# Gate matrix, top-k selection and sort of a PEER layer in 16-bit one-hot rows, and first gathers issued at seven places

## The chip, the cores and the metric

The kernel runs on one core of one Trainium2 chip. The metric is the device time of one execution in microseconds (us). A core has TensorE (PE, with its weight loads listed apart as PEld), VectorE (DVE), ScalarE (ACT), GpSimd (POOL) and SyncE (SP), which run their own instruction lists in order and wait for each other through semaphores, and 16 DMA engines that move data between HBM and the on-chip memory.

## The reference

One layer of a streaming encoder, over 256 positions of width 2048, all in f32. Its first half (adaptive normalization, a short convolution, latent attention, an output projection) is not touched by the change. The second half is a product-key retrieval over 128 x 128 = 16384 experts of one neuron each:

```python
q = (h @ w_q).reshape(bsz, seq, PEER_HEADS, 2, PEER_QDIM // 2)        # 8 heads, 2 halves of 128
scores = jnp.einsum('bshpd,hpnd->bshpn', q, sub_keys)                 # 128 keys per half
top_v, top_i = lax.top_k(scores, 16)
cand = top_v[..., 0, :, None] + top_v[..., 1, None, :]                # 16 x 16 candidates
best_v, best_i = lax.top_k(cand.reshape(..., 256), 16)
i1 = take_along_axis(top_i[..., 0, :], best_i // 16); i2 = take_along_axis(top_i[..., 1, :], best_i % 16)
expert = i1 * 128 + i2
gate = softmax(best_v)
a = einsum('td,tnd->tn', hx, u_tab[expert])
out = einsum('tn,tnd->td', gelu(a) * gate, v_tab[expert])
```

So each token picks 8 x 16 = 128 experts (i1, i2) with a gate each. The layer ends in a residual sum and a normalization.

## The kernel before

The tables `peer_u` and `peer_v` are not gathered per token. The kernel multiplies all 16384 rows of `peer_u` with all 256 tokens, 128 rows ("a block", index i1) at a time, and multiplies the activations with a dense gate matrix G[i1, i2, token] that is zero except at the chosen experts. The second table is then read row by row in a sorted order, so that rows that few tokens use share a matmul.

**Order of the work.** The whole is one Python program whose instructions are put in order, engine by engine, by a planner that goes by priority and by its own estimate of times; an instruction that is not marked by `keep` may be moved ahead of others. After the first half (to about 580 us) the main loop (from line 1154) runs over the 128 blocks. A block loads 1 MB of `peer_u` (`ru`), splits it on ACT into a high part (`hu`, line 198) and on DVE into a low part (`lu`, line 199), both with a raised priority (line 192), and does 48 matmuls (`pu`, lines 213, 214, 217): 16 slices of the high part with both halves of h2, then 16 of the low part. The last 16 need `lu`. A GELU (line 1160) writes the block's activations to a tile of eight blocks (`A`).

**Side work.** Between blocks, `pay(x)` advances a generator whose steps yield what they cost; each block pays 3.3 (`SIDE`) for the first 48 blocks, then, from block 51 on, 2.4 (`SORT_SIDE`). What is left of a generator at block 48 is drained there.

- `side_steps`, blocks 0 to 48, for each half of the tokens (tt): the 256 candidates, their top 16 (`top16`), the lookup of i1 and i2 by a comparison with `iota` over 8 x 16 x 16 elements (`eq`, line 902), a multiplication (line 906) and a reduction (line 908), the softmax, and a transpose on PE into `i1T`, `i2T`, `gT` (lines 921 to 923), one column per token. Then the one-hot rows: `oh_make` compares `iota` with four tokens' indices at a time, [128 selections, 4 tokens, 128] in f32, for i2 (into `work`, three places in turn) and i1 (into a tile of tag `e2`, four buffers), and ACT multiplies the latter by the gate (line 847). `oh_use`, two steps later (`HOLD`), makes one 128x128x128 f32 matmul per token (line 857), and ACT moves four tokens to a `stage` (line 859), of 16 tokens each. A full stage is written to HBM (`gd`, line 862) and reduced to its maximum on DVE (lines 865, 868).
- `sort_steps`, from block 51: from the maxima it sorts the 128 x 128 rows by which groups of 32 tokens use them (`tri`, `rank`), and turns ranks into a permutation by one-hot rows again (lines 1060 to 1076, `invert`): 32 chunks, each of four 128x256 16-bit matmuls (line 1057). The result is `perm_idx`.
- `ask(k)` reads the gate matrix of eight blocks back (`gg`, line 1100), `weigh(k)` multiplies it onto the activations on DVE (line 1106) and writes them to HBM (`actd`, line 1111). The first `ask` is at block 48, the first `weigh` at block 51.

**After the loop.** GpSimd gathers rows of v (`rv`, line 1145, 1 MB each) and of the activations (`mc`, line 1152) by `perm_idx`, and PE multiplies them (`po`, lines 1203 and 1211). Seven of the gathers of v (`EARLY`) are issued in the loop, all at block 118 (`EARLY_AT`), where the sort's remaining steps are also drained; five use tiles of the tag `A` (seven buffers), two the place of `work`.

Of the kernel before, what the change touches and what calls it, by code (L numbers as in the profile page):

```python
# [31 lines left out]
E2BUFS = 4  # L32
HOLD = 2
WRAW = 4
# [19 lines left out]
AHEAD = 8  # L54
EARLY_AT = NBLK - 10
RAWS = 11
# [74 lines left out]
def hybrid_block_kernel(  # L131
# [34 lines left out]
    def ps_tile(name):  # L166
# [76 lines left out]
    with tc.tile_pool(name="pre", bufs=1) as pre:  # L243
# [3 lines left out]
        def t8(name, dt=F32, shape=(128, 8, 256)):  # L247
            return pre.tile(list(shape), dt, tag="t8", name=name, bufs=6)

        vec = pre.tile([128, NVEC], F32, name="vec")  # L250
        nc.sync.dma_start(vec, vecs)
# [529 lines left out]
    def g8(name, shape, dt=F32):  # L781
# [9 lines left out]
           for i in range(2)]  # L791
    sifs = [tks[:, 1024 + i * 256:1280 + i * 256].rearrange("p (h k) -> p h k", k=16) for i in range(2)]

    def m1(name, dt=F32):
        return sp.tile([128, 256], dt, tag="m1", name=name, bufs=5)

# [34 lines left out]

    i1T, i2T, gT = [m1(n) for n in ("i1T", "i2T", "gT")]
    work = cst.tile([128, 4096], F32, tag="T2", name="work")
# [3 lines left out]
    def oh_make(tt, q):  # L837
        t = tt * 128 + q * 4
        it = iota.unsqueeze(1).to_broadcast([128, 4, 128])
        ohs = []  # L840
        for i, src in enumerate((i2T, i1T)):
            oh = e2(f"oh{tt}_{q}") if i else work[:, 2048 + 512 * ((32 * tt + q) % 3):][:, :512]
            oh = oh.rearrange("p (t i) -> p t i", t=4)
            V.tensor_tensor(oh, it, src[:, t:t + 4].unsqueeze(2).to_broadcast([128, 4, 128]), ALU.is_equal)  # L844
            ohs.append(oh)
        for j in range(4):
            S.activation(ohs[1][:, j], ohs[1][:, j], AF.Copy, scale=gT[:, t + j:t + j + 1])  # L847
        return ohs

    def oh_use(tt, q, ohs):  # L850
        tb, qq = divmod(q, TB // 4)
        if qq == 0:
            stages[tt, tb] = g8(f"stage{tt}_{tb}", (128, 128, TB))
        stage = stages[tt, tb]
        p = ps_tile(f"gps{tt}_{q}")
        for j in range(4):
            keep(PE.matmul(p[:, j * 128:(j + 1) * 128], lhsT=ohs[0][:, j], rhs=ohs[1][:, j],  # L857
                          start=True, stop=True))
        S.activation(stage[:, :, qq * 4:(qq + 1) * 4].rearrange("p i t -> p t i"),
                     p.rearrange("p (t i) -> p t i", t=4), AF.Copy)  # L860
        if qq == TB // 4 - 1:
            S.dma_start(gd[tt * (128 // TB) + tb], stage)
            gm = picked[:, 4 * tt + tb * TB // 32]
            if tb * TB % 32 == 0:
                V.tensor_reduce(gm, stage, AX.X, ALU.max)
            else:
                mx = e2(f"mx{tt}_{tb}")[:, :128]
                V.tensor_reduce(mx, stage, AX.X, ALU.max)
                V.tensor_tensor(gm, gm, mx, ALU.max)

    def side_steps():
# [5 lines left out]
        for tt in range(2):  # L877
# [16 lines left out]
            for which in range(2):  # L894
                if which == 0:
                    V.tensor_single_scalar(bs, bi, 4, ALU.logical_shift_right)
                else:
                    V.tensor_single_scalar(bs, bi, 15, ALU.bitwise_and)
                bf = tk[:, 1536:1664].rearrange("p (h k) -> p h k", k=16)
                V.tensor_copy(bf, bs)  # L900
# [5 lines left out]
                V.tensor_tensor(eq, eq, sfv[:, :, which].unsqueeze(2).to_broadcast([128, 8, 16, 16]),  # L906
                                ALU.mult)
                V.tensor_reduce(sel[:, which], eq, AX.X, ALU.add)
                yield 4.4
# [10 lines left out]
            ts_ = slice(tt * 128, (tt + 1) * 128)  # L920
            V.tensor_copy(i1T[:, ts_], pt[:, 0:128])
# [35 lines left out]
    def sort_steps():  # L957
        nk = len(CLASSES) + 1
        cls = work[:, 2048:2048 + 64 * nk].bitcast(BF).rearrange("p (k i) -> p k i", k=nk)
        flat = sp.tile([128, 512], BF, tag="m1", name="tri", bufs=5)  # L960
        tri, ones_bf, tot = flat[:, 0:128], flat[:, 128:256], flat[:, 256:256 + nk]
# [84 lines left out]
        V.tensor_single_scalar(ri, ri, 127, ALU.bitwise_and)  # L1046
        plo = work[:, 1024:1280].rearrange("p (c i) -> p c i", c=2)
        V.tensor_copy(plo[:, 0], ri)
        V.tensor_copy(plo[:, 1], rj)
        yield 5.0  # L1050
        pi = ps_tile("inv")
        it = iota.unsqueeze(1).to_broadcast([128, 4, 128])
        late = None

        def invert(ch, oh, vals):
            for i in range(4):
                keep(PE.matmul(pi[:, :256], lhsT=oh[:, 0, i], rhs=vals[:, i].rearrange("p a b -> p (a b)"),
                              start=(ch == 0 and i == 0), stop=(ch == 31 and i == 3)))

        for ch in range(32):  # L1060
            isl = slice(ch * 4, (ch + 1) * 4)
            oh = sp.tile([128, 2, 4, 128], BF, tag="e2", name=f"sl{ch}", bufs=E2BUFS)
            vals = sp.tile([128, 4, 2, 128], BF, tag="e2", name=f"sv{ch}", bufs=E2BUFS)
            for i in range(2):
                V.tensor_tensor(oh[:, i], it, plo[:, i, isl].unsqueeze(2).to_broadcast([128, 4, 128]),
                                ALU.is_equal)
            V.tensor_scalar(vals[:, :, 0], oh[:, 1], pidx, None, ALU.mult)
            V.tensor_tensor(vals[:, :, 1], oh[:, 1], iota[:, isl].unsqueeze(2).to_broadcast([128, 4, 128]),
                            ALU.mult)
            if late is not None:  # L1070
                invert(*late)
            late = (ch, oh, vals)
            yield 2.4
        yield 2.4
# [79 lines left out]
    for i1 in range(NBLK):  # L1154
# [260 lines left out]
```

## Time and profile before

| | us |
|---|---|
| median of three runs | 1780.37 |
| lowest and highest of them | 1776.81, 1781.57 |
| the profiled execution | 1774.11 |
| its span, first to last instruction | 1771.5 |
| PE busy (share of the span) | 1679.7 (95%) |
| PEld, weight loads | 1461.9 (83%) |
| DVE | 1210.0 (68%) |
| ACT | 761.3 (43%) |
| POOL | 297.5 (17%) |

The profile is that of one execution. Busy time counts a matmul from its start to its modelled end; matmuls overlap, so a busy PE may still lose time between starts, and the distance of starts says what a matmul costs. In a row of a group stand line, engine, operation, output<-inputs, shape and count, then busy time in total and mean ns of one, then the idle time of the engine ahead of them and what ended it. A line of the timeline or of the chain of waits starts with the time from the span's start and the duration, both in us.

### The profile page before, as it was taken

What the parts mean: (1) busy time and instruction counts of PE and PEld (TensorE: products, weight loads), DVE (VectorE), ACT (ScalarE), POOL (GpSimd) and SP (SyncE); (2) the same over time, 40 slices, a digit from 0 to 9 for tenths busy, and PEclk for the clock granted to TensorE, in tenths of its full rate; (3) what the DMA queues carried; (4) which work ended last, traced back from release to release, by engine and by line L of the source; (5) the groups of instructions that cost most, each with busy time, mean ns of one, the idle gap of its engine ahead of it and who ended that gap; (6) DMA issues with size and microseconds to landing.
All of it is one profiled execution on the core that took longest, in us unless ns stands there. A gap on an engine that the chain in (4) does not pass through costs nothing.

```text
span 1771.5 us, 29562 instructions
## 1 busy us (share of the span) xinstructions
PE 1679.7 (95%) x12526; PEld 1461.9 (83%) x12526; DVE 1210.0 (68%) x1621; ACT 761.3 (43%) x1013; POOL 297.5 (17%) x257
## 2 busy tenths in 40 slices
PE   3777999999999999999999999999999999999996
PEld 2667999989999999899999999999999854444542
DVE  6667978979867898898876697898754232312424
ACT  3224356534544449856884433333333232312322
POOL 0000000000000000000001000000030377777771
PEclk8888999999999999999999999999999999999999
DMA  9986887869854555545659887878888699999895
GB/s 392 385 336 214 327 299 269 316 250 348 311 213 165 192 194 191 206 166 191 223 214 337 305 296 262 298 286 309 289 300 335 216 386 382 347 383 344 343 371 232
DMA packets 77928, 505.93 MB, mean 286 GB/s; under 512 B 9472, under 2 KB 10112, under 8 KB 22496
## 3 DMA queue, kind: packets, MB, share of 16 engines
q1 hardware_dynamic: 44784, 319.82, 48.4%
q0 software_dynamic: 29712, 162.94, 25.1%
q10 hardware_dynamic: 3296, 21.24, 3.0%
q8 instruction: 100, 1.64, 0.4%
q14 instruction: 36, 0.29, 0.0%
HBM read 466.21 MB, written 37.75 MB: 284 GB/s over the span
## 4 chain that ended last, share of the span: by engine, by line
PE 85%; DVE 7%; ACT 4%; DMA 2%; issue 1%; POOL 1%; POOLq 0%; SPq 0%; ACTq 0%; DVEq 0%
PE pu L213 13%; PE pu L214 13%; PE pu L217 13%; PE po L1203 11%; PE po L1211 6%; PE gps L857 2%; PE pwin L213 2%; PE pwin L214 2%; PE pq L213 2%; PE pq L217 2%; PE pq L214 2%; DVE lwin L199 2%; PE pwout L213 1%; PE pwin L217 1%; PE pwout L214 1%; PE pwout L217 1%
## 5 line engine op out<-in xcount | busy, mean ns | idle before, releaser
L213 PE MATMUL pu<-h2hi,hu 128*128 128x256 f32 x2048 | 497.8, 285 | 0.0
L198 ACT ACTIVATE hu<-ru 128x2048 fp32r<-128x2048 f32 x128 | 245.5, 1918 | 364.4 <-PE pu L214 310.4
L213 PEld LDWEIGHTS pu<-h2hi,hu 128*128 128x128 f32 x2048 | 385.9, 188 | 0.6 <-issue 0.2
L199 DVE TENSOR_TENSOR lu<-ru,hu 128x2048 fp32r<-128x2048 f32 x128 | 292.9, 2289 | 134.4 <-ACT hu L198 134.2
L217 PE MATMUL pu<-h2hi,lu 128*128 128x256 f32 x2048 | 263.0, 281 | 0.0
L217 PEld LDWEIGHTS pu<-h2hi,lu 128*128 128x128 f32 x2048 | 251.3, 189 | 0.0
L214 PE MATMUL pu<-h2loT3a,hu 128*128 128x256 f32 x1024 | 249.7, 282 | 0.0
L214 PE MATMUL pu<-h2loT3b,hu 128*128 128x256 f32 x1024 | 248.2, 281 | 0.0
L1203 PE MATMUL po<-rv,mc 128*64 128x512 f32 (+2 forms) x1064 | 219.9, 595 | 5.1 <-PEq L1285 2.6
L214 PEld LDWEIGHTS pu<-h2loT3a,hu 128*128 128x128 f32 x1024 | 193.8, 189 | 0.2 <-issue 0.2
L214 PEld LDWEIGHTS pu<-h2loT3b,hu 128*128 128x128 f32 x1024 | 193.6, 189 | 0.0
L1203 PEld LDWEIGHTS po<-rv,mc 128*64 128x64 f32 (+2 forms) x1064 | 69.3, 129 | 144.5 <-issue 136.3
L1100 POOL DMA_DIRECT2D gg<-gd x16 | 18.7, 1170 | 928.5 <-DMA gd<-stage 928.3
L1152 POOL DMA_INDIRECT mc<-actd,perm_idx x109 | 134.4, 1233 | 37.1 <-issue 30.8
L1145 POOL DMA_INDIRECT rv<-in_peer_v_dram,perm_idx x107 | 125.3, 1171 | 65.5 <-issue 25.3
L204 DVE TENSOR_TENSOR lv<-rv,hv 128x2048 fp32r<-128x2048 f32 x24 | 55.1, 2295 | 117.5 <-ACT hv L203 117.4
L241 DVE SCALAR_TENSOR_TENSOR acc<-ada,cact,acc 128x2048 f32<-128x2048 f32 x45 | 105.7, 2349 | 5.9 <-DMA ada<-in_w_ada_dram 5.9
L203 ACT ACTIVATE hv<-rv 128x2048 fp32r<-128x2048 f32 x24 | 45.9, 1913 | 125.6 <-DMA rv<-in_peer_v_dram,perm_idx 98.1
L198 ACT ACTIVATE hwin<-rwin 128x2048 fp32r<-128x2048 f32 x33 | 63.1, 1916 | 81.3 <-DMA rwin<-in_w_in_dram 46.1
L204 DVE TENSOR_TENSOR third<-rv,third 128x2048 fp32r<-128x2048 f32 x12 | 27.5, 2294 | 89.5 <-ACT third L203 89.5
L847 ACT ACTIVATE oh<-oh,gT 128x128 f32<-128x128 f32 x256 | 80.9, 392 | 14.8 <-DVE oh L844 14.1
L213 PE MATMUL pwin<-hhi,hwin 128*128 128x256 f32 x336 | 84.7, 293 | 0.0
(522 smaller groups left out, 3048.1 us busy)
## 6 DMA issues: line engine op xcount, KB each, us to landing
ru<-in_peer_u_dram SPq DMA_DIRECT2D x128, 1024.0 KB, 5.3
ada<-in_w_ada_dram SPq DMA_DIRECT2D x96, 1024.0 KB, 6.7
rwin<-in_w_in_dram SPq DMA_DIRECT2D x33, 1024.0 KB, 6.1
rwout<-in_w_out_dram SPq DMA_DIRECT2D x16, 1024.0 KB, 7.3
rwq<-in_w_q_dram SPq DMA_DIRECT2D x16, 1024.0 KB, 6.5
gd<-stage ACTq DMA_DIRECT2D x16, 1024.0 KB, 5.3
gg<-gd POOLq DMA_DIRECT2D x16, 1024.0 KB, 11.1
actd<-A POOLq DMA_DIRECT2D x15, 1024.0 KB, 6.3
```

Of the source, the lines that this page charges most:

```text
L198: S.activation(hi, raw, AF.Copy)
L199: V.tensor_tensor(lo, raw, hi.bitcast(F32), ALU.subtract)
L204: V.tensor_tensor(lo, src, hi.bitcast(F32), ALU.subtract)
L213: PE.matmul(dst, lhsT=whi[:, sl], rhs=rhi[:, c], start=(c == sets[0][0]), stop=False)
L214: PE.matmul(dst, lhsT=whi[:, sl], rhs=rlo[:, c], start=False, stop=False)
L217: PE.matmul(dst, lhsT=wlo[:, sl], rhs=rhi[:, c], start=False, stop=(c == sets[-1][-1]))
L241: V.scalar_tensor_tensor(acc, raw, cact[:, k:k + 1], acc, ALU.mult, ALU.add)
L847: S.activation(ohs[1][:, j], ohs[1][:, j], AF.Copy, scale=gT[:, t + j:t + j + 1])
L1145: keep(nc.gpsimd.indirect_dma_start(raw, None, v_rows, index(main[n])))
L1152: keep(nc.gpsimd.indirect_dma_start(ms[-1][:, n % 8], None, actd[:, :], index(main[n])))
L1203: keep(PE.matmul(po[tt * 4 + d4][row:row + size], lhsT=m[:, at * size:(at + 1) * size], rhs=raw[:, d4 * 512:(d4 + 1) * 512], start=start, ...
L1211: keep(PE.matmul(po[tt * 4 + d4], lhsT=m[:, mi, tt * 128:(tt + 1) * 128], rhs=r[:, d4 * 512:(d4 + 1) * 512], start=False, stop=False, skip ...
```

## The change

The one-hot rows become 16-bit (bfloat16, which holds the integers 0 to 127 exactly), eight tokens at a time. Indices are stored twice, side by side, so that the innermost dimension of each operand of a comparison is two adjacent 16-bit elements. The gate stays exact to f32 by being split into three 16-bit parts (`gT[..., 0..2]`): the one-hot row of i1 is multiplied by all three on DVE in one operation, and PE adds three 16-bit matmuls per token. The multiplication on ACT goes. `HOLD` is 1. The product `og` has two places in `work`, both one-hot rows are tiles of tag `e2`. The lookup in the top-k selection compares and multiplies in 16 bits too. In the sort, 16 chunks of eight replace 32 of four, with two matmuls of 128 columns where one had 256. `iota` is 16-bit and is made by a count and a cast. The seven first gathers of v are issued at blocks 114, 116, ... 126, one each, and the sort's rest is drained at 114. The yields change with the step sizes: 2.6 per eight tokens instead of 1.2 per four, 2.0 instead of 1.0 behind the transpose, 2.6 per chunk of eight in the sort instead of 2.4 per chunk of four.

```diff
-HOLD = 2
+HOLD = 1
+OHB = 8
...
-EARLY_AT = NBLK - 10
+EARLY_AT = (114, 116, 118, 120, 122, 124, 126)
...
-    iota = cst.tile([128, 128], F32, name="iota")
-    nc.gpsimd.iota(iota, pattern=[[1, 128]], base=0, channel_multiplier=0,
-                   allow_small_or_imprecise_dtypes=True)
+    iota = cst.tile([128, 128], BF, name="iota")
...
+        V.tensor_copy(iota, count[:, :128])
...
-    i1T, i2T, gT = [m1(n) for n in ("i1T", "i2T", "gT")]
+    i1T, i2T = [sp.tile([128, T, 2], BF, tag="m1", name=n, bufs=2) for n in ("i1T", "i2T")]
+    gT = sp.tile([128, T, 3, 2], BF, tag="gT", name="gT")
+
+    def pairs_of(x):
+        return x.rearrange("p (a b) -> p a b", b=2)
+
+    def hot(dst, idx):
+        n = idx.shape[1]
+        V.tensor_tensor(dst.rearrange("p n (a b) -> p n a b", b=2),
+                        pairs_of(iota).unsqueeze(1).to_broadcast([128, n, 64, 2]),
+                        idx.unsqueeze(2).to_broadcast([128, n, 64, 2]), ALU.is_equal)
+
+    def twice(x):
+        return x.unsqueeze(2).to_broadcast([128, x.shape[1], 2])
...
     def oh_make(tt, q):
-        t = tt * 128 + q * 4
-        it = iota.unsqueeze(1).to_broadcast([128, 4, 128])
-        ohs = []
-        for i, src in enumerate((i2T, i1T)):
-            oh = e2(f"oh{tt}_{q}") if i else work[:, 2048 + 512 * ((32 * tt + q) % 3):][:, :512]
-            oh = oh.rearrange("p (t i) -> p t i", t=4)
-            V.tensor_tensor(oh, it, src[:, t:t + 4].unsqueeze(2).to_broadcast([128, 4, 128]), ALU.is_equal)
-            ohs.append(oh)
-        for j in range(4):
-            S.activation(ohs[1][:, j], ohs[1][:, j], AF.Copy, scale=gT[:, t + j:t + j + 1])
-        return ohs
+        t = tt * 128 + q * OHB
+        oh2, oh1 = [e2(f"oh{i}_{tt}_{q}").bitcast(BF).rearrange("p (t i) -> p t i", t=OHB) for i in (2, 1)]
+        og = work[:, 1024 + 1536 * (q % 2):2560 + 1536 * (q % 2)].bitcast(BF).rearrange("p (t c i) -> p t c i", t=OHB, c=3)
+        hot(oh2, i2T[:, t:t + OHB])
+        hot(oh1, i1T[:, t:t + OHB])
+        V.tensor_tensor(og.rearrange("p t c (a b) -> p t c a b", b=2),
+                        oh1.rearrange("p t (a b) -> p t a b", b=2).unsqueeze(2).to_broadcast([128, OHB, 3, 64, 2]),
+                        gT[:, t:t + OHB].unsqueeze(3).to_broadcast([128, OHB, 3, 64, 2]), ALU.mult)
+        return oh2, og
...
         for j in range(4):
-            keep(PE.matmul(p[:, j * 128:(j + 1) * 128], lhsT=ohs[0][:, j], rhs=ohs[1][:, j],
-                          start=True, stop=True))
+            for c in range(3):
+                keep(PE.matmul(p[:, j * 128:(j + 1) * 128], lhsT=ohs[0][:, t0 + j], rhs=ohs[1][:, t0 + j, c],
+                              start=(c == 0), stop=(c == 2)))
...
-                eq = g8(f"eq{tt}_{which}", (128, 8, 16, 16))
-                V.tensor_tensor(eq, bf.unsqueeze(3).to_broadcast([128, 8, 16, 16]),
-                                iota[:, :16].unsqueeze(1).unsqueeze(1).to_broadcast([128, 8, 16, 16]),
-                                ALU.is_equal)
+                eq = g8(f"eq{tt}_{which}", (128, 8, 16, 16), BF)
+                V.tensor_tensor(eq.rearrange("p h k (a b) -> p (h k) a b", b=2),
+                                bf.unsqueeze(2).to_broadcast([128, 128, 8, 2]),
+                                pairs_of(iota[:, :16]).unsqueeze(1).to_broadcast([128, 128, 8, 2]), ALU.is_equal)
...
-            V.tensor_copy(i1T[:, ts_], pt[:, 0:128])
-            V.tensor_copy(i2T[:, ts_], pt[:, 128:256])
-            V.tensor_copy(gT[:, ts_], pt[:, 256:384])
-            yield 1.0
-            for q in range(32):
+            V.tensor_copy(i1T[:, ts_], twice(pt[:, 0:128]))
+            V.tensor_copy(i2T[:, ts_], twice(pt[:, 128:256]))
+            left = tk[:, 1792:1920]
+            V.tensor_copy(gT[:, ts_, 0], twice(pt[:, 256:384]))
+            V.tensor_tensor(left, pt[:, 256:384], gT[:, ts_, 0, 0], ALU.subtract)
+            V.tensor_copy(gT[:, ts_, 1], twice(left))
+            V.tensor_tensor(left, left, gT[:, ts_, 1, 0], ALU.subtract)
+            V.tensor_copy(gT[:, ts_, 2], twice(left))
+            yield 2.0
+            for q in range(128 // OHB):
...
-                yield 1.2
+                yield 2.6
...
         def invert(ch, oh, vals):
-            for i in range(4):
-                keep(PE.matmul(pi[:, :256], lhsT=oh[:, 0, i], rhs=vals[:, i].rearrange("p a b -> p (a b)"),
-                              start=(ch == 0 and i == 0), stop=(ch == 31 and i == 3)))
+            for i in range(8):
+                for a in range(2):
+                    keep(PE.matmul(pi[:, a * 128:(a + 1) * 128], lhsT=oh[:, i], rhs=vals[a][:, i],
+                                  start=(ch + i + a == 0), stop=(ch == 15 and i == 7), skip_group_check=True))
...
-        if i1 == EARLY_AT:
+        if i1 == EARLY_AT[0]:
             for _ in side:
                 pass
-            for n in range(EARLY):
-                fetch_raw(n)
+        if i1 in EARLY_AT:
+            fetch_raw(EARLY_AT.index(i1))
```

More of the change, by code (lines that the diff above doesn't have):

```diff
@@ L248, in t8 @@
             return pre.tile(list(shape), dt, tag="t8", name=name, bufs=6)
+        count = s2("count")
+        nc.gpsimd.iota(count[:, :128], pattern=[[1, 128]], base=0, channel_multiplier=0,
+                       allow_small_or_imprecise_dtypes=True)
+        V.tensor_copy(iota, count[:, :128])
         vec = pre.tile([128, NVEC], F32, name="vec")
@@ L791, in hybrid_block_kernel @@
            for i in range(2)]
-    sifs = [tks[:, 1024 + i * 256:1280 + i * 256].rearrange("p (h k) -> p h k", k=16) for i in range(2)]
-    def m1(name, dt=F32):
-        return sp.tile([128, 256], dt, tag="m1", name=name, bufs=5)
+    sifs = [tks[:, 1024 + i * 128:1152 + i * 128].bitcast(BF).rearrange("p (h k) -> p h k", k=16)
+            for i in range(2)]
     def e2(name):
@@ L837, in oh_make, with oh_use, oh_four @@
     def oh_make(tt, q):
-        t = tt * 128 + q * 4
-        it = iota.unsqueeze(1).to_broadcast([128, 4, 128])
-        ohs = []
-        for i, src in enumerate((i2T, i1T)):
-            oh = e2(f"oh{tt}_{q}") if i else work[:, 2048 + 512 * ((32 * tt + q) % 3):][:, :512]
-            oh = oh.rearrange("p (t i) -> p t i", t=4)
-            V.tensor_tensor(oh, it, src[:, t:t + 4].unsqueeze(2).to_broadcast([128, 4, 128]), ALU.is_equal)
-            ohs.append(oh)
-        for j in range(4):
-            S.activation(ohs[1][:, j], ohs[1][:, j], AF.Copy, scale=gT[:, t + j:t + j + 1])
-        return ohs
-    def oh_use(tt, q, ohs):
+        t = tt * 128 + q * OHB
[7 more added lines that the diff above has]
+        return oh2, og
+    def oh_use(tt, b, ohs):
+        for half in range(OHB // 4):
+            oh_four(tt, b * (OHB // 4) + half, ohs, 4 * half)
+    def oh_four(tt, q, ohs, t0):
         tb, qq = divmod(q, TB // 4)
@@ L959, in sort_steps @@
         cls = work[:, 2048:2048 + 64 * nk].bitcast(BF).rearrange("p (k i) -> p k i", k=nk)
-        flat = sp.tile([128, 512], BF, tag="m1", name="tri", bufs=5)
+        flat = sp.tile([128, 512], BF, tag="m1", name="tri", bufs=2)
         tri, ones_bf, tot = flat[:, 0:128], flat[:, 128:256], flat[:, 256:256 + nk]
@@ L1046, in sort_steps @@
         V.tensor_single_scalar(ri, ri, 127, ALU.bitwise_and)
-        plo = work[:, 1024:1280].rearrange("p (c i) -> p c i", c=2)
-        V.tensor_copy(plo[:, 0], ri)
-        V.tensor_copy(plo[:, 1], rj)
+        plo = work[:, 1024:1280].bitcast(BF).rearrange("p (c i b) -> p c i b", c=2, b=2)
+        V.tensor_copy(plo[:, 0], twice(ri))
+        V.tensor_copy(plo[:, 1], twice(rj))
         yield 5.0
         pi = ps_tile("inv")
-        it = iota.unsqueeze(1).to_broadcast([128, 4, 128])
+        iota2 = work[:, 1408:1536].bitcast(BF).rearrange("p (i b) -> p i b", b=2)
@@ L1053, in sort_steps @@
+        V.tensor_copy(iota2, twice(iota))
         late = None
         def invert(ch, oh, vals):
-            for i in range(4):
-                keep(PE.matmul(pi[:, :256], lhsT=oh[:, 0, i], rhs=vals[:, i].rearrange("p a b -> p (a b)"),
-                              start=(ch == 0 and i == 0), stop=(ch == 31 and i == 3)))
[L1060 to L1069, printed above, removed]
+            for i in range(8):
+                for a in range(2):
+                    keep(PE.matmul(pi[:, a * 128:(a + 1) * 128], lhsT=oh[:, i], rhs=vals[a][:, i],
+                                  start=(ch + i + a == 0), stop=(ch == 15 and i == 7), skip_group_check=True))
@@ new lines, in sort_steps @@
+        for ch in range(16):
+            isl = slice(ch * 8, (ch + 1) * 8)
+            flats = ([work[:, 2048 + 512 * n:2560 + 512 * n] for n in range(4)] if ch % 2 else
+                     [e2(f"s{n}{ch}") for n in range(4)])
+            oh, oj, *vals = [x.bitcast(BF).rearrange("p (i j) -> p i j", i=8) for x in flats]
+            hot(oh, plo[:, 0, isl])
+            hot(oj, plo[:, 1, isl])
+            V.tensor_scalar(vals[0], oj, pidx, None, ALU.mult)
+            V.tensor_tensor(vals[1].rearrange("p i (a b) -> p i a b", b=2),
+                            oj.rearrange("p i (a b) -> p i a b", b=2),
+                            iota2[:, isl].unsqueeze(2).to_broadcast([128, 8, 64, 2]), ALU.mult)
```

6 lines of the change are left out of this document (3 added, 3 removed).

## The prediction

> **What bounds the kernel now.** I read the list of costliest groups first, then busy time in windows, then the waits inside them, then the timeline, down to single bursts of matmuls.
>
> Two stretches build the gate matrix from one-hot rows, 657 to 759 us (first 128 tokens) and 810 to 926 us (second). The windows view of both:
>
> ```profile
> 657.00:759.00 102.00, 97.22 (x817) 96.05 (x815) 83.69 (x92) 88.21 (x179) 0.00 (x0) 1.00 0.57 205
> 810.00:926.00 116.00, 112.03 (x952) 111.27 (x952) 93.68 (x97) 98.75 (x192) 0.00 (x0) 1.00 0.60 212
> ```
>
> Columns: stretch, length, then busy time of PE, weight loads, DVE, ACT, POOL, then granted clock, DMA share, GB/s. The clock is full and DMA at 0.6, so neither limits. PE is busy 209.25 of 218 us and idle 8.75; DVE is busy 177.4 (81%), ACT 187.0 (86%). So TensorE sets the time here, and its idle time adds to it. What it waits for, and what DVE waits for, in the waits view from 657 to 926 us:
>
> ```profile
> PE gps L857 <- ACT oh L847: 8.7, 9, 1.8
> DVE lu L199 <- ACT hu L198: 17.5, 12, 3.4
> DVE work L844 <- PE gps L857: 14.4, 14, 3.2
> DVE mx L868 <- ACT stage L859: 4.9, 3, 2.6
> DVE work L865 <- ACT stage L859: 3.1, 5, 1.1
> ```
>
> (Columns: total in us, number of waits, longest.) All PE idle time there waits for one thing: the scaling of one-hot rows by the gate on ScalarE, line 847. Outside these stretches the `peer_u` blocks follow each other without gaps. The chain of waits has their last sixteen matmuls every 5.68 us:
>
> ```profile
> 592.27 1.89 PE pu L217 x16
> 597.95 1.89 PE pu L217 x16
> 669.89 2.68 PE gps L857 x24
> ```
>
> So each microsecond of matmul removed before 1402 us, where the last block ends, shortens the run. After it comes the expert product, fed by gathers of v; nothing of its matmuls changes.
>
> **The change part by part.**
>
> *One-hot matmuls.* Now, the groups:
>
> ```profile
> L857 PE MATMUL gps<-oh,work 128*128 128x128 f32 x512 | 67.4, 280 | 8.7 <-ACT oh L847 8.7
> L844 DVE TENSOR_TENSOR work<-iota,i2T 128x512 f32<-128x512 f32 x64 | 43.9, 688 | 14.4 <-PE gps L857 14.4
> L844 DVE TENSOR_TENSOR oh<-iota,i1T 128x512 f32<-128x512 f32 x64 | 43.2, 686 | 0.0
> L847 ACT ACTIVATE oh<-oh,gT 128x128 f32<-128x128 f32 x256 | 80.9, 392 | 14.8 <-DVE oh L844 14.1 <-ACT oh L847 0.7
> L906 DVE TENSOR_TENSOR eq<-eq,tks 128x2048 f32<-128x2048 f32 x4 | 9.2, 2288 | 0.0
> L1068 DVE TENSOR_TENSOR sv<-sl,iota 128x512 bf16<-128x512 bf16 x32 | 21.9, 685 | 0.0
> L1067 DVE TENSOR_SCALAR sv<-sl,pidx 128x512 bf16<-128x512 bf16 x32 | 11.3, 353 | 0.9
> L865 DVE TENSOR_REDUCE work<-stage 128x128 f32<-128x2048 f32 x8 | 18.3, 2284 | 3.1 <-ACT stage L859 3.1
> ```
>
> Each of 256 tokens is one f32 matmul, run as two instructions: 512. Mean durations overlap, so I take the distance of starts. In the chain 24 of them take 2.68 us: 0.1117 each, 57.2 us in all. After the change a token is three 16-bit matmuls of 128 columns: 768. The trace has this shape in the ranking of the sort, timeline from 1011.5 us:
>
> ```profile
> 1011.81 0.39 PE L1031 MATMUL rank<-work,tri 128*128 128x512 bf16 x1
> 1012.04 0.39 PE L1034 MATMUL rank<-tri 128*128 128x128 bf16 x4
> 1012.23 0.37 PE L213 MATMUL pu<-h2hi,hu 128*128 128x256 f32 x1
> 1012.44 0.28 PE L214 MATMUL pu<-h2loT3a,hu 128*128 128x256 f32 x1
> ```
>
> and the summary of that line (shortest, median, longest duration in ns):
>
> ```profile
> L1034 PEld LDWEIGHTS <-tri x24: 97/98/100, 1011.8 to 1048.8; 128*128 128x128 bf16 x24
> L1034 PE MATMUL rank<-tri x24: 219/220/220, 1012.0 to 1048.8; 128*128 128x128 bf16 x24
> ```
>
> Four take 0.39 us, the last alone 0.22, so starts are (0.39 - 0.22)/3 = 0.057 us apart, each with its own weight load. At that distance 768 take 43.8 us. It is a bound from below, since it is a run of only four, behind a long matmul that can hide a load. From above: a weight load lasts 98 ns, and if loads did not overlap 768 would take 75.3 us. I take 0.057, because the loads in that row do overlap.
>
> The Trainium skill speaks against it: "TensorE: Matmul & The Clock Gate", section Back-to-back issue gap, states about 81 ns per matmul for sustained pairs of load and matmul at 128 columns. By that figure the 768 would be an estimated 62 us, more than now. No row here shows a long run of this shape.
>
> The first f32 matmul behind 16-bit ones is late: from the last L1034 (1012.04 + 0.39 - 0.22 = 1012.21) to L214 at 1012.44 are 0.23 us, where 0.057 and one `peer_u` distance of 5.68/48 = 0.118 make 0.175. That is 0.055 per burst; at some 28 bursts, 1.5 us.
>
> *DVE in these stretches.* It loses 128 comparisons of 512 elements (43.9 + 43.2 = 87.1 us) and gains 64 comparisons of 1024 and 32 multiplications of 3072, all operands 16 bits. Between 512 elements (687 ns) and 2048 (2288 ns), a two-tensor operation costs 1.043 ns per further element. No row shows a two-tensor operation with only 16-bit operands. Upper bound, as f32: 1221 and 3357 ns. Lower: L1067, all 16 bits, takes 353 ns for 512 elements, half of 687; half the steps gives 687 and 1756 ns. I take the lower, as L1067 is the only row with 16 bits throughout. That makes 44.0 + 56.2 = 100.2 us, 13.1 more than now. The three copies behind the transpose become seven operations; a copy now is
>
> ```profile
> 658.95 0.28 DVE L921 COPY i1T<-selT 128x128 f32<-128x128 f32 x1
> ```
>
> and with doubled outputs some 0.4 each: about 2 us more per half, 4 in all. DVE then needs 177.4 + 13.1 + 4 = 194.5 us in stretches that PE would leave at 218 - 57.2 + 43.8 + 1.5 = 206 us: 94% busy. It fits, but with little room. The top-k selection also gets cheaper: four comparisons and four multiplications of 2048 go from 2288 to an estimated 1221 ns, 8.5 us of DVE, outside the stretches and hidden behind PE. The reductions stay.
>
> *ACT.* The 80.9 us of line 847 go; what remains is 106 us in 218. This is the only thing PE waited for. But the multiplication moves to DVE, at 94%, and PE waits for that instead. I let half of the 8.75 us return: a gain of 4.4, between none and 8.75 (the visible idle time; a little more hides in the modelled ends).
>
> *Order.* Eight tokens per step cost 2.6 of budget instead of 2 x 1.2, and the total of the side work goes from 153.6 to 162.0 of 3.3 per block: from 46.5 blocks to 49.1, with the rest drained at block 48. The first weighting of activations at block 51 needs the matrix written and read back:
>
> ```profile
> gd<-stage ACTq DMA_DIRECT2D x16, 1024.0 KB, 5.3
> gg<-gd POOLq DMA_DIRECT2D x16, 1024.0 KB, 11.1
> ```
>
> (KB, and us from issue to landing.) DVE's timeline there:
>
> ```profile
> 937.79 2.29 DVE L199 TENSOR_TENSOR lu<-ru,hu 128x2048 fp32r<-128x2048 f32 x1
> 939.99 2.29 DVE L1106 TENSOR_TENSOR A<-A,gg 128x2048 f32<-128x2048 f32 x1
> ```
>
> L1106 now starts as the read lands. With the work 2.6 blocks (15 us) later it may hold DVE, and behind it the low parts of the next blocks (L199), which PE needs after 32 of a block's 48 matmuls and which run about a block (5.7 us) ahead: a cost of 0 to 9 us. I take 0, since the low parts carry a priority of their own (line 192) and can be put ahead of it.
>
> *Sort.* The inverse goes from 128 matmuls of 256 columns to 256 of 128. Timeline: four now take 0.61 us with the last 0.273,
>
> ```profile
> 1089.59 0.61 PE L1057 MATMUL inv<-sv,sl 128*128 128x256 bf16 x4
> ```
>
> 0.112 apart, 14.4 us in all; afterwards 256 x 0.057 plus 16 bursts x 0.055 is 15.5: 1.1 more. Its DVE work stays about equal, with fewer instructions.
>
> *Gathers.* Seven fetches issued together at block 118 now go out one per two blocks, 114 to 126. POOL's timeline:
>
> ```profile
> 1315.06 1.73 POOL L1145 DMA_INDIRECT rv<-in_peer_v_dram,perm_idx  x1 [0.30 <-issue]
> ...
> 1395.15 0.84 POOL L1111 DMA_DIRECT2D actd<-A  x1 [24.46 <-DVE A L1106]
> 1400.14 1.01 POOL L1152 DMA_INDIRECT mc<-actd,perm_idx  x1 [4.16 <-DMA actd<-A]
> ```
>
> PE lost nothing to the burst, so spreading gains nothing. The last fetch now stands on POOL behind the write at 1395 and shares engines with it; the gathers of activations wait for that write. Cost between 0 and 5.3 us, the landing time of 1 MB in the row of `gd`; I take 1, since PE has other products to do when the gathers start. That the sort has ended by block 114: its budget falls by 35 of 2.4 per block, so it ends earlier than now. The 16-bit count at the start hides behind the first loads.
>
> *Sum*, against the profiled execution's 1774.1 us (span 1771.5 and 2.6 around it): -57.2 + 43.8 + 1.5 - 4.4 + 1.1 + 1.0 = -14.2, so 1759.9. The median of the runs shown, 1780.4, lies 6.3 above the profiled execution; on that scale I forecast 1766.
>
> **The rivals.**
>
> *No change: DVE takes ACT's place.* DVE needs 194.5 us, and of its waits those on ACT (17.5 + 4.9 + 3.1 = 25.5) could stay. Then the stretches last 220 us as they do now, and the sum is +2 + 1.1 + 1 = 4 over: 1778 by the profile's scale, 1784. For it: 94% busy, in order, with reductions of 2.28 us (L865) ahead of low parts; and the product is held in two buffers, so that the multiplication two steps on waits for PE, as the comparisons do now (14.4), with low parts queued behind it. Against: ACT loses 43% of its work, so waits on ACT should shrink.
>
> *Slower: the 16-bit operations on DVE run at f32 speed.* Then they take 64 x 1.221 + 32 x 3.357 = 185.6 us, DVE needs 280 us in the stretches, 62 more than the stretches last now: 1838 by the profile, 1844. It decides from a multiplication of about 2.5 us on, where DVE's 194.5 us become 218. For it: L1068, which writes 16 bits but reads the f32 `iota` beside a 16-bit operand, takes 685 ns like f32. Against: L1067.
>
> *Slower: weight loads.* If long runs are paced by loads of 98 ns, 768 take 75.3 and the inverse 25.1 + 0.9: -57.2 + 75.3 + 1.5 - 4.4 + 11.6 + 1 = +28: 1808. At the skill's 81 ns it would be an estimated 10 over instead. For it: a load of 98 ns outlasts the 57 ns between starts, so it must always begin ahead; against it: four starts did lie 57 ns apart.
>
> **How the numbers follow.** Forecast 0.66; no change through DVE 0.16; DVE at f32 speed 0.06; weight loads 0.06; other mishaps, the weighting and the gathers among them, 0.06, halved between a smaller gain and none. A measurement of this kernel tells from no change what differs by more than 0.3%, 5 us. Faster: 0.66 + 0.03 = 0.69; same 0.17; slower 0.14. The forecast's own range: all waits gone and a little hidden idle time, 1756, to the 9 us of the weighting, 1775. For eight in ten I add the no-change case and some loss: 1754 to 1787.
>
> **What would show it.** 768 matmuls of the one-hot line with starts 0.056 to 0.06 apart; multiplications of 3072 near 1.76 us; ACT below 55% in the stretches; the two stretches some 16 us shorter; the end stage as long as now. Wrong, if matmuls of that line lie 0.08 or more apart, if the multiplication takes over 2.5 us, if PE's waits for DVE in the stretches exceed 9 us, or if the end stage moves by over 3 us.

## The result, and the profile after

The changed kernel takes 1763.69 us (median of five runs, 1760.77 to 1765.6); the kernel before took 1776.81 in the same comparison (five runs, 1776.48 to 1781.57). The ratio is 0.9916, 95% interval 0.9898 to 0.9933: faster by 0.7 to 1.0%. The forecast was 1766, the range 1754 to 1787. The profiled execution after took 1763.69 us, its span 1761.9, against 1774.11 and 1771.5 before: 9.6 us less in the span.

The windows view of the two stretches with one-hot work after the change (the matmuls of 26 blocks of `peer_u` and 63 of the 64 evictions of gate matrices lie in them, as in the 218 us of before):

```profile
661.00:757.00 96.00, 95.65 (x992) 94.99 (x991) 95.01 (x79) 58.86 (x57) 0.00 (x0) 1.00 0.65 221
813.00:911.00 98.00, 98.00 (x1039) 97.47 (x1038) 97.48 (x83) 62.03 (x61) 0.00 (x0) 1.00 0.65 230
```

The columns are those of before. The stretches have shrunk from 218 to 194 us. PE is busy 193.65 us of them, DVE 192.5: both are full. The waits view from 657 to 945 us (total, number, longest, in us):

```profile
DVE lu L198 <- ACT hu L197: 14.5, 6, 3.4
DVE A L1131 <- DMA gg<-gd: 9.0, 1, 9.0
...
PE pu L216 <- DVE lu L198: 5.1, 1, 5.1
```

The waits of PE on the scaling are gone, and nothing has come in their place in the stretches. What is new is the wait of the first weighting, L1131, for its read, and PE behind it. The groups:

```profile
L874 PE MATMUL gps<-work,oh 128*128 128x128 bf16 x768 | 47.4, 219 | 0.4 <-DVE work L857 0.4
L857 DVE TENSOR_TENSOR work<-oh,gT 128x3072 bf16<-128x3072 bf16 x32 | 56.0, 1754 | 0.2
L841 DVE TENSOR_TENSOR oh<-iota,i1T 128x1024 bf16<-128x1024 bf16 x32 | 22.0, 688 | 0.2
L841 DVE TENSOR_TENSOR oh<-iota,i2T 128x1024 bf16<-128x1024 bf16 x32 | 21.9, 685 | 0.0
L925 DVE TENSOR_REDUCE tk<-eq 128x128 f32<-128x2048 bf16 x4 | 9.1, 2282 | 0.0
L919 DVE TENSOR_TENSOR eq<-tk,iota 128x2048 bf16<-128x2048 bf16 x4 | 4.9, 1225 | 0.0
```

A comparison of 1024 elements takes 0.69 us, the multiplication of 3072 takes 1.754 (1.756 was forecast), the top-k comparison 1.225 (1.221). The reduction from 16 bits takes 2.28 us, as from f32. The bursts of matmuls in PE's timeline:

```profile
672.25 2.85 PE L874 MATMUL gps<-work,oh 128*128 128x128 bf16 x48
...
680.68 1.51 PE L874 MATMUL gps<-work,oh 128*128 128x128 bf16 x24
```

The last of a burst takes 0.22, so the 48 start (2.85 - 0.22)/47 = 0.056 us apart, and so do the 24: 768 are 43.0 us. DVE's timeline around the first weighting:

```profile
922.92 0.50 DVE L1004 TENSOR_SCALAR work<-work 128x128 bf16<-128x128 f32 x3
932.40 2.29 DVE L1131 TENSOR_TENSOR A<-A,gg 128x2048 f32<-128x2048 f32 x1 [8.97 <-DMA gg<-gd]
934.61 2.28 DVE L198 TENSOR_TENSOR lu<-ru,hu 128x2048 fp32r<-128x2048 f32 x1
```

DVE stands for 9 us in front of the weighting, and the low part that PE needs stands behind it. PE's timeline shows the sixteen matmuls that need a low part, a block earlier and behind that wait:

```profile
926.00 2.06 PE L216 MATMUL pu<-h2hi,lu 128*128 128x256 f32 x16
...
936.94 3.78 PE L216 MATMUL pu<-h2hi,lu 128*128 128x256 f32 x16 [5.10 <-DVE lu L198]
```

Behind the wait they also run slower: starts lie 0.213 us apart where they were 0.118, and the granted clock is 0.50 from 936.9 to 941 us and 1.00 from 925 to 932. And DVE's timeline near the start, where the first normalization factor is copied (`r`), first of the kernel before, then of the changed one:

```profile
18.71 0.16 DVE L339 SCALAR_TENSOR_TENSOR n0v<-n0v,n0r 128x2 f32<-128x2 f32 x1
...
20.57 0.42 DVE L370 COPY r<-n0b 128x256 f32<-128x256 f32 x1 [1.31 <-PE n0b L347]
```

```profile
19.66 0.75 DVE L406 SCALAR_TENSOR_TENSOR acc<-ada,cact,acc 128x512 f32<-128x512 f32 x1
20.33 0.15 DVE L342 SCALAR_TENSOR_TENSOR n0v<-n0v,n0r 128x2 f32<-128x2 f32 x1
20.45 0.75 DVE L406 SCALAR_TENSOR_TENSOR acc<-ada,cact,acc 128x512 f32<-128x512 f32 x1
...
22.78 0.42 DVE L373 COPY r<-n0b 128x256 f32<-128x256 f32 x1 [1.31 <-PE n0b L350]
```

The small steps of the reciprocal square root now stand between multiply-adds of 0.75 us, and `r` is 2.2 us later. So there were four questions: how much the removed waits were worth, what bounds the stretches now, what the weighting costs, and whether the start's delay reaches the end.

### The profile page after: what moved, and what is told of

It reads as the page before. It is cut to its first block, busy times and chain, and to the rows that moved or that the text cites. A ratio compares the mean times of both kernels' runs of the same rounds, so it can differ in the third digit from the quotient of the medians.

```text
span 1761.9 us, 29917 instructions
## 1 busy us (share of the span) xinstructions
PE 1668.4 (95%) x12910; PEld 1453.2 (82%) x12910; DVE 1185.6 (67%) x1535; ACT 695.0 (39%) x757; POOL 290.8 (17%) x257
## 4 chain that ended last, share of the span: by engine, by line
PE 80%; DVE 6%; DMA 4%; issue 4%; POOL 4%; ACT 2%; another core or an unknown queue 0%; POOLq 0%; SPq 0%; DVEq 0%; ACTq 0%
PE pu L212 13%; PE pu L216 13%; PE pu L213 13%; PE po L1228 8%; PE po L1236 3%; PE gps L874 2%; POOL mc L1177 2%; PE pwin L212 2%; PE pwin L213 2%; PE pq L212 2%; PE pq L216 2%; PE pq L213 2%; POOL rv L1170 2%; DVE lwin L198 2%; PE pwout L212 2%
## 5 line engine op out<-in xcount | busy, mean ns | idle before, releaser
L198 DVE TENSOR_TENSOR lu<-ru,hu 128x2048 fp32r<-128x2048 f32 x128 | 293.3, 2292 | 168.9 <-ACT hu L197 168.1
L1177 POOL DMA_INDIRECT mc<-actd,perm_idx x109 | 128.2, 1176 | 36.4 <-issue 31.1
L198 DVE TENSOR_TENSOR lwin<-rwin,hwin 128x2048 fp32r<-128x2048 f32 x33 | 75.5, 2289 | 10.7 <-ACT hwin L197 9.0
```

The lines of the kernel that those rows point to most:

```text
L198: V.tensor_tensor(lo, raw, hi.bitcast(F32), ALU.subtract)
L1177: keep(nc.gpsimd.indirect_dma_start(ms[-1][:, n % 8], None, actd[:, :], index(main[n])))
```

## The experiments

All are edits of the changed kernel, unless said otherwise. The table shows each profile by four times (us): the start of the loop over `peer_u` (first `pu` matmul), the distance from the start of block 13 to that of block 49 (it holds all one-hot work), the whole loop, and the end stage behind it; the last column is the ratio of the times to the kernel before, with its 95% interval.

| kernel | loop starts | blocks 13 to 49 | loop | end stage | ratio |
|---|---|---|---|---|---|
| before | 580.9 | 274.8 | 821.1 | 369.5 | |
| changed | 584.9 | 250.0 | 804.7 | 372.2 | 0.9916 (0.9898, 0.9933) |
| e1 cast later | 582.0 | 250.0 | 804.6 | 371.1 | 0.9918 (0.9904, 0.9932) |
| e2 first weighting later | 581.2 | 250.0 | 797.3 | 369.6 | 0.9883 (0.9866, 0.9900) |
| e3 both | 581.0 | 250.0 | 797.8 | 370.7 | 0.9882 (0.9865, 0.9898) |
| e4 gathers together | 582.1 | 250.0 | 805.5 | 367.9 | 0.9923 (0.9910, 0.9937) |
| e5 gate by step 0 | 586.1 | 297.6 | 845.8 | 376.1 | 1.0147 (1.0117, 1.0177) |
| e6 one part | 583.7 | 249.2 | 801.1 | 374.6 | 0.9889 (0.9858, 0.9920) |
| e7 before, no scaling | 582.5 | 262.1 | 808.5 | 372.0 | 0.9900 (0.9872, 0.9928) |
| e8 before again | 582.0 | 274.8 | 821.2 | 374.5 | 0.9997 (0.9982, 1.0011) |
| e9 before, with count | 585.8 | 274.8 | 821.2 | 370.7 | 1.0005 (0.9996, 1.0014) |
| e10 16-bit iota at once | 581.9 | 250.0 | 803.7 | 374.6 | 0.9906 (0.9883, 0.9929) |
| e11 e10 and e2 | 582.2 | 250.0 | 797.3 | 371.2 | 0.9850 (0.9834, 0.9865) |
| e12 e11, two parts | 582.3 | 235.8 | 783.1 | 367.1 | 0.9787 (0.9767, 0.9807) |

Where the work is the same, blocks 13 to 49 agree within 0.1 us between profiles and the loop within about 1; the start and the end stage differ by several us between executions, so a difference of two profiles there shows little.

**What were the waits for ScalarE worth?** The kernel before without the multiplication by the gate:

```diff
-        for j in range(4):
-            S.activation(ohs[1][:, j], ohs[1][:, j], AF.Copy, scale=gT[:, t + j:t + j + 1])
```

> The kernel before without the multiplication of one-hot rows by the gate on ScalarE (the gate matrix holds ones at the chosen experts); the f32 matmuls stay. It asks what the waits for that multiplication cost alone. Theory (all of the waits were the loss, and the starts of matmuls show a little more than the 8.75 us that the waits view lists): TensorE has no waits above 1 us in the two stretches, starts stay 0.112 apart, and the run takes 9 to 13 us less than the kernel before, ratio 0.993 to 0.995. Rival (half of it turns into waits for DVE, as I let it in the sum): 4.4 us less, 0.9975. Second rival (the waits were hidden, none of it returns): 1.000.

Its one-hot matmuls, and the stretches by windows (the second ends here at 920):

```profile
L855 PE MATMUL gps<-oh,work 128*128 128x128 f32 x512 | 61.2, 275 | 0.0
```

```profile
657.00:759.00 102.00, 102.00 (x879) 102.00 (x878) 86.16 (x93) 60.96 (x57) 0.00 (x0) 1.00 0.60 211
810.00:920.00 110.00, 110.00 (x948) 110.00 (x947) 96.19 (x117) 66.01 (x63) 0.00 (x0) 1.00 0.65 225
```

PE has no idle time left, with the same 512 f32 matmuls. Blocks 13 to 49 take 274.8 - 262.1 = 12.7 us less, where the waits view had listed 8.7. By these blocks the theory holds, and the half that I let in the sum does not. By the ratio it falls short: 0.993 to 0.995 was expected, and 0.990 asks for more than 12.7 of 1780 (0.9929, just outside its interval); where the rest lies, the profiles don't show. So of the 24.8 us by which the change shortens these blocks, 12.7 are to be had without any 16-bit matmul, and the other 12.1 come with the rest of the change.

**What bounds the stretches now?** One of the three matmuls per token:

```diff
-            for c in range(3):
+            for c in range(1):
...
-                              start=(c == 0), stop=(c == 2)))
+                              start=True, stop=True))
```

> The changed kernel with one of the three matmuls per token; the second and third part of the gate are still made by DVE but left out of the gate matrix. It asks what bounds the two stretches now. It takes 512 x 0.056 = 28.7 us from TensorE and nothing from DVE. Theory (DVE, 97 to 99 per cent busy there, is as full as TensorE): TensorE's time turns into waits for DVE (low parts and products), and the run gains under 5 us, ratio to the kernel before 0.989 to 0.992. Rival (TensorE alone bounds, as the prediction's sum has it, and DVE's work spreads): a gain of 20 to 28.7 us, ratio 0.976 to 0.980.

Its stretches by windows, and its waits from 657 to 945 us:

```profile
661.00:757.00 96.00, 87.39 (x776) 86.03 (x775) 93.94 (x79) 59.27 (x57) 0.00 (x0) 0.96 0.62 223
813.00:908.00 95.00, 83.91 (x717) 82.54 (x716) 92.29 (x78) 58.08 (x55) 0.00 (x0) 0.93 0.62 221
```

```profile
PE gps L874 <- DVE work L857: 19.6, 10, 5.4
```

Of 28.7 us taken from PE, blocks 13 to 49 give 0.8: PE waits for products of DVE instead, 19.6 us of it, and DVE is busy 186 of the 191 us shown. Some 6 us more go to matmuls of `peer_u` that start further apart than in the changed kernel, at a granted clock of 0.96 and 0.93. (The loop is 3.6 shorter, the rest of it at the first weighting.) The theory holds: DVE bounds the stretches within a microsecond of PE. "No change through DVE", the rival with the chance of 0.16, missed by this little.

**Are the pairs needed?** The multiplication with the gate part read by step 0:

```diff
-        V.tensor_tensor(og.rearrange("p t c (a b) -> p t c a b", b=2),
-                        oh1.rearrange("p t (a b) -> p t a b", b=2).unsqueeze(2).to_broadcast([128, OHB, 3, 64, 2]),
-                        gT[:, t:t + OHB].unsqueeze(3).to_broadcast([128, OHB, 3, 64, 2]), ALU.mult)
+        V.tensor_tensor(og, oh1.unsqueeze(2).to_broadcast([128, OHB, 3, 128]),
+                        gT[:, t:t + OHB, :, 0].unsqueeze(3).to_broadcast([128, OHB, 3, 128]), ALU.mult)
```

> The changed kernel, but the multiplication by the gate reads each gate part as one element 128 times (innermost step 0) instead of as pairs of two adjacent copies; all results are the same. It asks what the pairs are worth, and where the rival 'DVE at f32 speed' would have led. Theory (the pairs are what makes the operation run at the 16-bit speed): the multiplication of 3072 elements takes about 3.36 us instead of 1.75, 32 of them are 51 us more on a DVE that is 97 to 99 per cent busy there, TensorE waits for DVE in both stretches, and the run is 40 to 51 us longer than the changed kernel, about 1.02 of the kernel before. Rival (16-bit operands are enough, pairs or not): 1.75 us and no change, ratio 0.992.

```profile
L857 DVE TENSOR_TENSOR work<-oh,gT 128x3072 bf16<-128x3072 bf16 x32 | 107.2, 3351 | 0.1
L873 PE MATMUL gps<-work,oh 128*128 128x128 bf16 x768 | 55.2, 235 | 34.6 <-DVE work L857 34.6
```

With 16-bit operands throughout, but one of them without pairs, the operation takes 3351 ns, the f32 figure. DVE's 51 us more make blocks 13 to 49 47.7 longer; 6.7 come back behind them, where PE no longer waits at the first weighting, and the loop is 41.0 longer. The theory holds. The Trainium skill ("Vector Engine (DVE) Microarchitecture Reference", section Performance modes) asks for the doubled speed of an operation with two tensors that all operands have two bytes and an innermost step of one; the 1754 and 3351 ns agree.

**The first weighting, the start and the gathers.** First the weighting alone:

```diff
-            weighs.setdefault(at, []).append(k)
+            weighs.setdefault(at + (2 if k == 0 else 0), []).append(k)
```

> The first weighting of activations (k = 0) is asked of DVE two blocks later; its read of the gate matrix is issued where it was. Theory (DVE stands in front of the weighting for 9.0 us until the read lands, and the low part behind it makes PE lose 7.0 us in block 52): the wait of L1131 for the read is below 1 us, no block near 931 to 937 loses over 1 us, the run takes about 1756.7. Rival (the wait only moves, since the later weighting of 2.3 us then stands ahead of another low part): PE loses 2 to 3 us there, 1759. Second rival (PE's loss there is made up later, since blocks are bound by the loads of peer_u): 1763.7.

```profile
922.15 2.28 DVE L198 TENSOR_TENSOR lu<-ru,hu 128x2048 fp32r<-128x2048 f32 x1
...
925.44 2.28 DVE L198 TENSOR_TENSOR lu<-ru,hu 128x2048 fp32r<-128x2048 f32 x1
933.20 2.29 DVE L1131 TENSOR_TENSOR A<-A,gg 128x2048 f32<-128x2048 f32 x1 [5.48 <-DMA gg<-gd]
935.41 4.49 DVE L198 TENSOR_TENSOR lu<-ru,hu 128x2048 fp32r<-128x2048 f32 x2
```

DVE still waits 5.5 us for the read, against the expectation of under 1, but two low parts more stand ahead of it, and PE no longer waits for any. The loop is 804.7 - 797.3 = 7.4 us shorter, of which the listed wait was 5.1; the slower matmuls behind it account for some 2. The ratio lies below those of the two kernels beside it that keep the early weighting (e1, e4), their intervals apart. The theory's price holds, its way only in part: here DVE's wait stays and PE's goes, with the low parts ahead.

Next the start: the count and the cast moved behind the first stage's loads, and both edits together.

```diff
-        count = s2("count")
-        nc.gpsimd.iota(count[:, :128], pattern=[[1, 128]], base=0, channel_multiplier=0,
-                       allow_small_or_imprecise_dtypes=True)
-        V.tensor_copy(iota, count[:, :128])
         vec = pre.tile([128, NVEC], F32, name="vec")
...
+        count = s2("count")
+        nc.gpsimd.iota(count[:, :128], pattern=[[1, 128]], base=0, channel_multiplier=0,
+                       allow_small_or_imprecise_dtypes=True)
+        V.tensor_copy(iota, count[:, :128])
```

> The count and its cast to 16 bits stand in the program just ahead of the convolution instead of at the start; all else is the changed kernel. Theory (the 4.4 us that the changed kernel loses before the loop over peer_u come from the order on DVE: the steps of the reciprocal square root and the copy of r stand behind two more multiply-adds): r is copied near 20.6 us again instead of 22.8, the first loop matmul starts near 581 instead of 585.2, the run takes about 1759.5. Rival (that loss comes from the loads or is noise between profiled executions): first loop matmul at 585 still, 1763.7. Second rival (it comes back in the first stage, but a later load or the end stage, which is bound by transfers, takes it away): 581 and 1763.7.

> Both edits: the cast later and the first weighting two blocks later. Theory: the two losses lie in series on TensorE, so the gains add: 4.4 + 7.0 = 11.4 below the changed kernel, about 1752.3, a ratio to the kernel before of 0.985 to 0.986. Rival (one of them is taken back by the end stage): 1756 to 1760.

In e1 the first `pin` matmul starts at 37.3 us, as before (37.6; 39.8 in the changed kernel, 39.7 in e4 on the same chip). But the loop starts at 582.0, and at 582.1 in e4: nothing is left of the 2.4, and the ratio of 0.9918 is the changed kernel's. The order came back as the theory had it, the time did not. The windows views of e4 and of e1 show where most of it went:

```profile
160.00:200.00 40.00, 36.54 (x291) 35.61 (x289) 39.55 (x56) 17.57 (x19) 0.00 (x0) 0.96 0.83 310
160.00:200.00 40.00, 36.32 (x277) 35.34 (x275) 38.23 (x57) 16.26 (x17) 0.00 (x0) 0.91 0.81 295
```

The granted clock is 0.91 there in e1, and 0.96 in e4 as in all the other profiles but e3's; matmuls that started 1.7 us ahead of e4's at 168.8 are level by 193. Narrower windows put the granted clock at 0.50 from 177.5 to 184.3 us in e1 and from 179.2 to 182.5 in e4: 3.5 us more at half clock, which is that 1.7. In e3 it is 0.91 too. The gain did not add up: e3 is where e2 is.

To see the start without a moved cast, three kernels ran on one chip: the kernel before; the same with the changed kernel's count and copy, in f32; and the changed kernel with `iota` in 16 bits from GpSimd at once. A fourth adds the later weighting to the last.

```diff
     iota = cst.tile([128, 128], BF, name="iota")
+    nc.gpsimd.iota(iota, pattern=[[1, 128]], base=0, channel_multiplier=0,
+                   allow_small_or_imprecise_dtypes=True)
...
-        count = s2("count")
-        nc.gpsimd.iota(count[:, :128], pattern=[[1, 128]], base=0, channel_multiplier=0,
-                       allow_small_or_imprecise_dtypes=True)
-        V.tensor_copy(iota, count[:, :128])
```

> The kernel before, unchanged, on the chip of the next three runs: it gives their start and end stage a profile to stand against, and shows what the comparison makes of no change. Both theories: ratio 1.000 within 0.002, first loop matmul at 581 to 583, end stage 369 to 375 us.

> The kernel before with one part of the change alone: its iota comes from a count and a copy on DVE (in f32) where the changed kernel has them. Theory (the planner then puts DVE's first operations in the changed kernel's order, and that is the loss of the start): r is copied near 22.8 us, the first matmul of pin starts 2 to 2.5 us later than in the unchanged kernel beside it, and the run is 2 to 4.4 us longer, ratio 1.001 to 1.0025. Rival (what the start loses is given back later, as it was in the kernel with the cast moved): 2 us later at pin, nothing at the first loop matmul, ratio 1.000.

> The changed kernel with iota written in 16 bits by GpSimd at once, without the count and without the cast on DVE; DVE's order up to the loop is that of the kernel before. Theory (the start's loss is the order): pin and the first loop matmul start within 0.5 us of the unchanged kernel's, against 2 to 3 us later with the cast; the run is 2 us below the changed kernel, ratio 0.990. Rival (given back by the clock granted between 160 and 200 us, 0.91 instead of 0.96 in the kernel with the cast moved): pin as before, first loop matmul 1.5 us later, ratio 0.9916.

> The 16-bit iota without cast, and the first weighting two blocks later. Theory (two losses in series): 7 us below the run with the 16-bit iota alone, ratio 0.985 to 0.987. Rival (only the weighting counts): 0.988, as with the later weighting alone.

The copy of `r` in DVE's timeline, of e9 and of e10:

```profile
23.01 0.42 DVE L372 COPY r<-n0b 128x256 f32<-128x256 f32 x1 [1.32 <-PE n0b L349]
```

```profile
20.63 0.42 DVE L371 COPY r<-n0b 128x256 f32<-128x256 f32 x1 [1.32 <-PE n0b L348]
```

The count with its copy delays `r` in the kernel before too (23.0 against 20.5 in e8); with the 16-bit `iota` at once the order returns. All profiles agree: in the six with the count and its copy at the start, `r` is copied at 22.7 to 23.2 us and `pin` starts at 39.1 to 40.9; in the eight others at 20.1 to 20.6 and at 37.1 to 38.5 (e10 has the 38.5, 1.0 later than e8 where 0.5 was allowed). So the delay of some 2 us up to `pin` is the order on DVE, and that is shown. What is left of it later is not: e9's loop starts 3.8 us behind e8's, but e2, with the same count and copy, starts it at 581.2. The six start it 2.1 us later on average, and the two groups overlap. In the time, e9 against e8 (1.0005 and 0.9997) and e10 against the changed kernel (0.9906 and 0.9916) have intervals that overlap; only e11, at 0.985, lies below e2, its like with the early cast, with intervals just apart and on another chip. e11 also lies 0.56% below e10, intervals apart: the weighting again, 6.4 us of it in the loop. The rival that only the weighting counts (0.988) lies outside e11's interval. At 0.985 it beats both kernels.

Last the gathers, seven at block 118 as before:

```diff
-EARLY_AT = (114, 116, 118, 120, 122, 124, 126)
+EARLY_AT = NBLK - 10
```

> Only the gathers of v as in the kernel before: all seven issued at block 118, and the rest of the sort drained there. Theory (spreading them gains nothing, and its cost, which I put at 1 us, is that the last one shares engines with the first gathers of activations): the end stage, 371.9 us in the changed kernel against 369.5 before, goes back by 1 to 2.4, the run takes 1761 to 1763. Rival (spreading hides a burst that would delay the loads of the last blocks): blocks 118 to 127 lose 2 to 5 us and the run takes 1766 to 1769. Second rival (no effect, the end stage is bound by its 30 and more later gathers): 1763.7 within 1.

The end stage is 367.9 us against 369.6 to 371.1 in the three kernels beside it, the loop 0.9 longer than e1's, the time the same within the intervals. Nothing here shows a gain from spreading; whether it costs 1 or 2 us can't be told, since kernels with one and the same end stage range from 367.1 to 376.1.

**Both engines relieved.** Since PE and DVE are both full, time should come back only where both have less. Two gate parts, on top of e11:

```diff
-    gT = sp.tile([128, T, 3, 2], BF, tag="gT", name="gT")
+    gT = sp.tile([128, T, 2, 2], BF, tag="gT", name="gT")
...
-            V.tensor_tensor(left, left, gT[:, ts_, 1, 0], ALU.subtract)
-            V.tensor_copy(gT[:, ts_, 2], twice(left))
...
-            for c in range(3):
+            for c in range(2):
```

> The kernel with the 16-bit iota and the later first weighting, and with two gate parts instead of three: the third part (what is left of the gate behind 16 bits of its fraction) is left out of the gate matrix. It takes 256 x 0.056 = 14.3 us from TensorE and, by the distance between the comparison of 1024 elements and the multiplication of 3072, (1.754 - 0.687)/2 x 32 = 17 us from DVE, in the same stretches. Theory (TensorE and DVE are both full there, so that time comes back only when both get shorter; 28.7 us from TensorE alone gave some 4): the loop over peer_u gets 13 to 15 us shorter, from 797.3 to about 783, the ratio to the kernel before falls from 0.985 to 0.977. Rival (a third thing sets the pace by now, the loads of peer_u or the transfers between stages): 0 to 5 us, ratio 0.982 to 0.985.

```profile
L855 DVE TENSOR_TENSOR work<-oh,gT 128x2048 bf16<-128x2048 bf16 x32 | 39.0, 1217 | 0.3
L872 PE MATMUL gps<-work,oh 128*128 128x128 bf16 x512 | 33.1, 220 | 0.5 <-DVE work L855 0.5
```

14.3 us less on PE and 17 less on DVE shorten blocks 13 to 49 by 14.2 and the loop by 14.2: all that PE was spared, where 28.7 from PE alone gave 0.8. The theory holds. Less work on DVE alone was not tried; that it would gain nothing is argued from PE, busy 193.65 of 194 us. (This kernel's gate carries 16 significant bits, not 24.)

## Why the prediction was right, and where it was not

The time came out 2 us below the forecast. That it was so near is partly luck: the waits returned 8.3 us more than the sum had, the first weighting cost some 7 that the sum had at nothing, and the delay at the start was left out. What made the change faster, fewer microseconds of one-hot matmuls and no wait for ScalarE, was named rightly.

- **One-hot matmuls, -57.2 + 43.8.** Right: 0.056 us between starts, 43.0 in all, in bursts of 24 and 48 and not only of four. The loads of 98 ns overlap throughout, and the rival of paced weight loads falls. The Trainium skill's figure of about 81 ns ("TensorE: Matmul & The Clock Gate", section Back-to-back issue gap) is not borne out here.
- **Bursts, +1.5.** About 2, by difference only: 12.1 came with the rest of the change, where 57.2 - 43.0 are 14.2.
- **Waits for ScalarE, -4.4.** The mis-sized term: e7 measures -12.7. Two things were wrong in "I let half of the 8.75 us return". PE does not wait for DVE (0.4 us), and the 8.75 of the waits view understated the loss, because a matmul's modelled end hides part of each gap; I had put that at "a little". The lower end of my own range was loose as well: all waits gone is 1762 on the scale of the 1766, and 1756 needs 6 us of hidden idle time, where e7 returned 4.0 beyond the listed ones.
- **DVE.** The durations were right within 5 ns, but the reason, 16 bits throughout, lacked a condition: e5 has 16 bits throughout, but no pairs in one operand, and takes 3351. Nearly right was the need: 194.5 us forecast, 192.5 measured. The share was not, 94% forecast and 99% found, because the stretches became 194 us long and not 206. ACT's share is 62% and not below 55, since the stretches are shorter and since I took its need too low (106 us, found 120.9): I subtracted all 80.9 of line 847, but part of that time ran beside other operations of ACT; in the trace of before, ACT without line 847 is still busy 120.6 us of these stretches. The stretches got 24 us shorter and not 16. That each microsecond of matmul removed shortens the run held for the kernel before; in the changed one e6 shows that it no longer does.
- **The first weighting, 0 of 0 to 9.** The step that failed: "the low parts carry a priority of their own and can be put ahead of it". They were not; L1131 was put ahead of L198, the read landed 9 us late and PE lost some 7 us (e2: 7.4, e11 against e10: 6.4), 5.1 of them as a wait and some 2 at half clock behind it. The mechanism and the upper bound were named, the wrong end was chosen.
- **The 16-bit count, "hides behind the first loads".** Its cast takes 0.23 us itself, but changed the planner's order: `r` and the first `pin` matmul come some 2 us later. I looked for the work's duration and not for what it displaces. How much of it reaches the end stays open.
- **Sort, +1.1.** 16 bursts in place of 32 cost about 1 more. Right.
- **Gathers, +1.0.** End stage 2.7 longer in the profiles; within the spread of that stage, so neither shown nor refuted.

By the traces the loop's terms make -14.2 + 2.1 - 12.7 + 1.0 + 7.4 = -16.4, measured -16.4; the 2.1 is itself a difference, so this is bookkeeping and no test. With 4.1 later at its start and 2.7 longer at its end that is -9.6 of span. The ratio says some 15 us, and the kernel before's profiled execution was below all of its runs in that comparison: part of the 4.1 and 2.7 is probably the spread of executions. The order of the rivals was right; the nearest, DVE, was closer than 0.16 suggests.

## What to carry to other kernels

Where a pipeline's engines wait for a third, test the removal of that wait alone: the listed idle time is a lower bound (8.7 listed, 12.7 returned), and it may be half of a change that has another name. When a change takes work from one engine and gives it to another, compute the new share against the new, shorter stretch: much the same need, 194.5 us forecast and 192.5 found, was 94% of the one and 99% of the other, and from there on relief of TensorE alone gave 0.8 us of 28.7, relief of both 14.2 of 14.3. When a stage gets shorter or later against its schedule, look at the first instruction that reads its result through memory, and at what stands behind that instruction on its engine.

## What the runs showed of the hardware

Pairs of a weight load of 98 ns and a 16-bit matmul of 128 columns keep 56 ns between starts over 48 in a row. A multiplication of 3072 16-bit elements by a second tensor took 1754 ns with pairs of adjacent elements in every operand, and 3351 with one operand read by step 0. Two kernels whose first matmuls came 2.4 us earlier were granted a clock of 0.91 instead of 0.96 from 160 to 200 us and lost some 1.7 us there; e10 and e11, with the same order, were granted 0.96, so it isn't the order alone, and what it is stays open. In e6, where PE was kept waiting in the stretches, its granted clock was 0.96 and 0.93, and 1.00 where it was not. A wait of PE can cost more than its length: behind the 5.1 us at the first weighting the granted clock was 0.50 for at least 4 us, and matmuls started 0.213 us apart instead of 0.118.
